# Three of twelve modulation blocks issued later, behind an output projection

## The chip, the cores and the metric

The kernel runs on one core of a Trainium2 chip. The metric is device time in microseconds (us) from launch to end; lower is better. A core has a matrix engine (TensorE, PE in the profile, with PEld for its weight loads), a vector engine (VectorE, DVE), a scalar engine (ScalarE, ACT), GpSimd (POOL) and SyncE (SP), which here issues nearly all DMAs. Each engine takes its instructions in the order in which the program lists them.

## What is computed

Two networks of two layers each on 256 rows of 1024 features. The first is causal attention and a gated convolutional MLP. The second takes the first one's result as `x` and a second sequence, the context, and each of its layers is modulated by six vectors of 1024 numbers, for the latent sequence (`ml`) and for the context (`mc`):

```python
for i in range(DEPTH):
    ml = jnp.split(s_lat @ w_ada[i] + b_ada[i], 6, axis=-1)
    mc = jnp.split(s_ctx @ w_ada[i] + b_ada[i], 6, axis=-1)
    u_lat = modulate(h_lat, g_pre_mix[i], ml[0], ml[1])
    ...
    h_lat = h_lat + ml[2] * rms_norm_2(o_lat, g_post_mix[i])
    f_lat = sqrelu_mlp(modulate(h_lat, g_pre_ff[i], ml[3], ml[4]), w_ff1[i], w_ff2[i])
    h_lat = h_lat + ml[5] * rms_norm_2(f_lat, g_post_ff[i])
```

`w_ada[i]` is 1024 by 6144, in float32. The vectors depend on two small inputs alone, so they can be made at any time before they are used.

## The kernel before

All large products are made in three passes of float32r: a weight tile (`raw`, 512 KB) is loaded by SP, ScalarE makes its high part (`whi`, L265), DVE or POOL the low part (`wlo`, L269), and TensorE multiplies. Matmuls write PSUM banks, of which there are four groups: A, B, C and D. D is one bank.

The method `ada` (L751 on) makes the modulation in twelve blocks of 512 columns. A block is eight loads of 256 KB (tile `adaw`, L775, on SP), eight matmuls (L778) whose left side is 32 columns wide, so that four of them use different column strips of the array, a copy to SBUF on ScalarE (`asb`, L780), four transposes (`adaT`, L784), and a reduction and an addition on DVE (L786, L787). The trace has two records for each of these float32 matmuls, 16 for a block. In the lane `sd`, which the change touches, the eight loads share six buffers (tag `mid`), and both PSUM tiles of a block use bank D, so blocks run one after another. The last of the three blocks (index 9) has two more small DVE instructions, which fold the norm's gain into its result.

Blocks 0 to 3 of the second layer serve its first norm, 4 and 5 its first gate, 6 to 9 the norm ahead of its MLP (shift and scale), 10 and 11 its last gate. `side` traces blocks 0 to 9 and then `setup_odd`, a table of biases made in eight steps (`chk` loads on POOL, transposing matmuls `cb`, L1097), in the lane `sd` too.

The program text is a priority list, not the order of issue. A planner fixes each engine's order ahead of the run, with a model of how long everything takes: of what is ready on an engine it takes what was traced first. Thus blocks traced ahead of the first network's second MLP (`conv_ffn(1)`) mix with it and with the steps around it. `behind(steps)` traces steps so that their TensorE instructions come after the last projection matmul traced so far (`self.last`) in TensorE's order. Nothing else of the steps is held by it; their DMAs start when a buffer is free.

In `run`, the order of tracing is: the first network's layer 0, the context's first mixer, blocks of layer 0's modulation, the first network's layer 1 attention, `side`, `conv_ffn(1)`, then `second_block`. In that, `lat_out` is an output projection followed by `post` (a scaled residual), `lat_mlp` a norm (`nT` transposes, L370) followed by an MLP of 16 steps (`f`, L308 to L310, and `acc`, L746 to L748). `context2` makes the context's projection and MLP beside the latent mixer and then its next norm, and blocks 10 and 11 already stand behind the second `lat_out`, in the lane `cx`.

```python
    def behind(self, steps):
        with self.tc.issue_after(self.last.ins):
            for _ in steps:
                pass
```

Of the kernel before, what the change touches and what calls it, by code (L numbers as in the profile page):

```python
# [188 lines left out]
class Net:  # L189
# [865 lines left out]
            pass  # L1055

    def side(self):
        for _ in itertools.chain(self.ada(self.sd, 1, 1, range(10)), self.setup_odd(self.sd)):
            pass

    def behind(self, steps):
# [85 lines left out]
    def rwkv_group(self, L, s, feat, put, ve, p0, n, tz, sg, vd, fill):  # L1147
# [86 lines left out]
        for pi in range(n):  # L1234
# [64 lines left out]
            for c in range(8):  # L1299
                for d in range(2):  # L1300
                    for h, hr in enumerate(hs):
                        nc.tensor.matmul(sc[h][hs[side(h, d)], c], BK[hr, d, c], AR[hr, d, c], start=True, stop=True)
# [5 lines left out]
            for h in range(2):  # L1308
                q0 = (pi * 2 * 2 + h) * 8
                nc.sync.dma_start(nm[q0:q0 + 8].rearrange("c s t -> s c t"), G[lows[h], h, :, 0:32])  # L1310
                o = lows[side(h, 1)]
                nc.vector.transpose(nt[o], G[o, h, :, 0:32])
                nc.sync.dma_start(nm[q0 + 16:q0 + 24].rearrange("c s t -> s c t"), nt[o])

            BG = L.mid([128, 2, 256], name="ic"), L.mid([128, 2, 256], name="kd")
            for d in range(2):
                step()
                bg = BG[d].rearrange("p a (c t) -> p (a c) t", t=64)
                nc.vector.tensor_tensor(bg, BK[:, d], gC[:, d, pi].unsqueeze(2).to_broadcast([128, 8, 64]), op=OP.mult)
                ps = L.pB("bkt")  # L1320
                pv = ps.rearrange("p (c f) -> p c f", c=4)
                for c in range(4):
                    nc.tensor.transpose(pv[:, c], bg[:, 2 * c:2 * c + 2].rearrange("p c t -> p (c t)"), self.ident)
                for e in range(2):
                    for h in range(2):
                        eng = nc.scalar.copy if e == 0 else nc.vector.tensor_copy
                        eng(BKt[hs[side(h, d)], d, e::2], pv[hs[e], :, hs[h]])
# [437 lines left out]
    def second_block(self, x):  # L1765
        L = self.lat
        end = self.last
        act = self.even_mix(L, 0, x)
        self.lat_out(0, act, x)
        odd = self.context2(end)  # L1770
        self.lat_mlp(0, x)
        self.behind(odd)
        act = self.odd_mix(x)
        self.lat_out(1, act, x)
        self.behind(self.ada(self.cx, 1, 2, range(10, 12)))
        self.lat_mlp(1, x)
# [62 lines left out]
```

## Time and profile before

| | us |
|---|---|
| Median of 3 runs (2070.97 to 2075.08) | 2072.32 |
| The profiled execution | 2065.47 |
| Its span, first to last instruction | 2063.3 |
| TensorE busy | 1898.4 (92%) |
| DVE busy | 1378.0 (67%) |
| ACT busy | 1026.3 (50%) |
| POOL busy | 852.4 (41%) |

The stages that matter, from the trace: the first network's last output projection ends at 741 us; the norm ahead of `conv_ffn(1)` lasts to 758.7; `conv_ffn(1)` runs to 996, with the context's recurrent scan beside it; the second block's mixer runs to 1435; its first `lat_out` ends at 1462.6; the norm of `lat_mlp(0)` lasts to 1485.8 and its matmuls to 1666. Blocks 7, 8 and 9 of the second layer's modulation run from 743.6 to 792. In the views, PEclk is the granted clock of TensorE as a share of its full 2.4 GHz, so 0.5 is 1.2 GHz; "x" is a count of records, and what stands in brackets behind "<-" ended an idle time.

### The profile page before, as it was taken

The page shows a single profiled execution, that of the slowest core. Times are in us where ns is not written, and L with a number is a line of the kernel's source. Part 1 is how long each engine was busy: PE and PEld are TensorE (multiplying, and loading weights), DVE is VectorE, ACT ScalarE, POOL GpSimd, SP SyncE. Part 2 cuts the span into 40 slices and gives each one's busy share as a digit, 9 for nine tenths or more (in the row PEclk, how much of TensorE's full clock was granted, in tenths as well). Part 3 has the DMA queues.
Part 4 walks back from the last instruction along what each step waited for, and adds up shares of the span by engine and source line. Part 5 has one row for each costly group of instructions (what it writes and reads, how often), then busy time and mean ns, then how long its engine had stood idle before and what let it go on. Part 6 is the DMA issues. An engine that isn't in the chain of part 4 may idle for free. (4 is left out here: it accounts for less than half of the span.)

```text
span 2063.3 us, 37705 instructions
## 1 busy us (share of the span) xinstructions
PE 1898.4 (92%) x14178; PEld 1580.8 (77%) x14178; DVE 1378.0 (67%) x2919; ACT 1026.3 (50%) x1990; POOL 852.4 (41%) x557
## 2 busy tenths in 40 slices
PE   6989999989999889999898888998699999998998
PEld 4567868888666458899797878887699977777997
DVE  5475378876788646786778888678744468645444
ACT  4455455545454335465555544554544444654443
POOL 3235544593332444454544433113255554013453
PEclk9999999999999999999999999999799999999999
DMA  9857555445454665575472653327555436225562
GB/s 344 311 176 229 159 171 168 146 153 178 127 191 160 199 196 171 183 232 170 133 255 95 184 152 117 91 61 215 183 174 195 164 100 232 82 93 164 180 198 72
DMA packets 270815, 351.08 MB, mean 170 GB/s; under 512 B 43150, under 2 KB 195469, under 8 KB 270632
## 3 DMA queue, kind: packets, MB, share of 16 engines
q1 hardware_dynamic: 267992, 343.32, 51.8%
q0 software_dynamic: 1968, 4.33, 0.7%
q8 instruction: 112, 1.84, 0.4%
q10 hardware_dynamic: 672, 1.02, 0.1%
q14 instruction: 71, 0.58, 0.1%
HBM read 334.04 MB, written 14.55 MB: 169 GB/s over the span
## 5 line engine op out<-in xcount | busy, mean ns | idle before, releaser
L269 POOL TENSOR_TENSOR wlo<-raw,whi 128x1024 fp32r<-128x1024 f32 (+2 forms) x344 | 705.3, 2061 | 1042.6 <-ACT whi L265 920.2
L265 ACT ACTIVATE whi<-raw 128x1024 fp32r<-128x1024 f32 (+2 forms) x600 | 508.2, 883 | 140.7 <-issue 34.0
L269 DVE TENSOR_TENSOR wlo<-raw,whi 128x1024 fp32r<-128x1024 f32 (+1 forms) x256 | 356.7, 1395 | 112.5 <-ACT whi L265 101.4
L310 PE MATMUL f<-ah,wlo 128*128 128x256 f32 x768 | 222.3, 290 | 13.5 <-DVE wlo L269 6.9
L308 PE MATMUL f<-ah,whi 128*128 128x256 f32 x768 | 220.6, 288 | 2.8 <-DVE T L1343 1.8
L309 PE MATMUL f<-al,whi 128*128 128x256 f32 x768 | 222.2, 290 | 0.0
L746 PE MATMUL acc<-whi,hh 128*128 128x512 f32 x432 | 168.8, 393 | 2.1 <-ACT hh L461 2.1
L747 PE MATMUL acc<-wlo,hh 128*128 128x512 f32 x432 | 169.3, 392 | 0.0
L748 PE MATMUL acc<-whi,hl 128*128 128x512 f32 x432 | 165.3, 390 | 0.4 <-DVE hl L462 0.4
L310 PEld LDWEIGHTS f<-ah,wlo 128*128 128x128 f32 x768 | 150.0, 195 | 17.2 <-DVE wlo L269 8.5
L308 PEld LDWEIGHTS f<-ah,whi 128*128 128x128 f32 x768 | 150.0, 196 | 5.7 <-ACT whi L265 2.5
L309 PEld LDWEIGHTS f<-al,whi 128*128 128x128 f32 x768 | 150.1, 196 | 2.9 <-issue 0.8
L1596 ACT ACTIVATE r<-f 128x512 f32<-128x512 f32 x48 | 28.6, 596 | 191.2 <-PE f L310 191.2
L1597 DVE TENSOR_TENSOR r<-r 128x512 f32<-128x512 f32 x48 | 34.6, 721 | 131.8 <-ACT r L1596 131.6
L293 PE MATMUL prj<-wlo,ah 128*128 128x512 f32 (+1 forms) x272 | 107.1, 395 | 2.7 <-DVE wlo L269 1.6
L292 PE MATMUL prj<-whi,ah 128*128 128x512 f32 (+1 forms) x272 | 107.4, 400 | 0.4 <-DVE bt L499 0.4
L310 PE MATMUL g<-ah,wlo 128*128 128x256 f32 x352 | 101.4, 288 | 5.8 <-POOL wlo L269 5.8
L294 PE MATMUL prj<-whi,al 128*128 128x512 f32 (+1 forms) x272 | 105.4, 396 | 1.2 <-DVE al L383 1.2
L778 PE MATMUL ada<-adaw,kept 128*32 128x512 f32 x384 | 98.8, 640 | 7.3 <-DMA adaw<-in_w_ada_dram 6.9
L308 PE MATMUL g<-ah,whi 128*128 128x256 f32 x352 | 101.9, 290 | 0.4 <-DVE kept L786 0.4
L308 PE MATMUL up<-ah,whi 128*128 128x256 f32 x352 | 102.2, 290 | 0.0
L310 PE MATMUL up<-ah,wlo 128*128 128x256 f32 x352 | 101.3, 288 | 0.9 <-POOL wlo L269 0.9
(473 smaller groups left out, 4825.8 us busy)
## 6 DMA issues: line engine op xcount, KB each, us to landing
raw<-in_w_ff_dram SPq DMA_DIRECT2D x128, 512.0 KB, 4.1
raw<-in_w_up_dram SPq DMA_DIRECT2D x88, 512.0 KB, 4.6
adaw<-in_w_ada_dram SPq DMA_DIRECT2D x144, 256.0 KB, 5.4
raw<-in_w_ff_dram SPq DMA_DIRECT2D x128, 256.0 KB, 4.6
raw<-in_w_in_dram SPq DMA_DIRECT2D x48, 512.0 KB, 4.7
raw<-in_w_down_dram SPq DMA_DIRECT2D x44, 512.0 KB, 4.5
adaw<-in_w_ada_dram SPq DMA_DIRECT2D x24, 512.0 KB, 7.6
raw<-in_w_out_dram SPq DMA_DIRECT2D x24, 512.0 KB, 5.1
```

Of the source, the lines that this page charges most:

```text
L265: nc.scalar.activation(hi, raw, AF.Copy)
L269: eng.tensor_tensor(lo, raw, hi.bitcast(F32), op=OP.subtract)
L292: nc.tensor.matmul(ps[t][:, :n], ah, wh[:, k], start=st, stop=False)
L293: nc.tensor.matmul(ps[t][:, :n], ah, wl[:, k], start=False, stop=False)
L294: self.last = nc.tensor.matmul(ps[t][:, :n], al, wh[:, k], start=False, stop=en)
L308: nc.tensor.matmul(pv[:, j], wh[:, k % a, c], ah, start=first, stop=False, skip_group_check=skip)
L309: nc.tensor.matmul(pv[:, j], wh[:, k % a, c], al, start=False, stop=False, skip_group_check=skip)
L310: nc.tensor.matmul(pv[:, j], wl[:, k % a, c], ah, start=False, stop=k == 7, skip_group_check=skip)
L746: nc.tensor.matmul(acc[t][n], hh[:, k, c], wh[:, n], start=st, stop=False)
L747: nc.tensor.matmul(acc[t][n], hh[:, k, c], wl[:, n], start=False, stop=False)
L748: self.last = nc.tensor.matmul(acc[t][n], hl[:, k, c], wh[:, n], start=False, stop=en)
L778: nc.tensor.matmul(ps[32 * j:32 * j + 32], self.sT[:, k], raw[:, k - kb], start=k < 4, stop=k >= 4)
```

## The change

`side` traces blocks 0 to 6 only, and blocks 7 to 9 are traced in `second_block` right after the first `lat_out`, through `behind`, in the same lane with the same buffers. No operation is added or removed.

```diff
     def side(self):
-        for _ in itertools.chain(self.ada(self.sd, 1, 1, range(10)), self.setup_odd(self.sd)):
+        for _ in itertools.chain(self.ada(self.sd, 1, 1, range(7)), self.setup_odd(self.sd)):
             pass
...
         act = self.even_mix(L, 0, x)
         self.lat_out(0, act, x)
+
+        self.behind(self.ada(self.sd, 1, 1, range(7, 10)))
         odd = self.context2(end)
         self.lat_mlp(0, x)
         self.behind(odd)
```

## Rows read from the trace of the kernel before

**Rows 1.** Stretch, length, busy time: PE, PEld, DVE, ACT, POOL; PEclk, DMA share, GB/s.
```profile
741.00:758.60 17.60, 11.13 (x52) 4.23 (x50) 11.14 (x30) 8.12 (x18) 7.18 (x12) 0.81 0.69 214
758.60:793.00 34.40, 34.40 (x311) 23.71 (x312) 15.77 (x40) 13.82 (x29) 6.60 (x6) 1.00 0.61 196
1462.00:1486.00 24.00, 7.88 (x36) 6.72 (x35) 20.36 (x73) 14.18 (x32) 4.00 (x2) 0.58 0.34 113
...
880.00:940.00 60.00, 58.29 (x405) 54.48 (x404) 50.69 (x68) 35.88 (x50) 29.72 (x14) 1.00 0.71 222
1486.00:1530.00 44.00, 44.00 (x301) 41.08 (x301) 23.42 (x27) 21.64 (x28) 22.48 (x8) 0.99 0.59 189
```

**Rows 2.** TensorE's waits from 758.7 to 996 us: total, times, longest.
```profile
PE acc L746 <- ACT hh L461: 1.7, 1, 1.7
PE yT L1465 <- DVE Y L1460: 1.7, 1, 1.7
...
```

**Rows 3.** Busy by stretch, `ada` alone: PE, PEld, ACT; clock, DMA share, GB/s.
```profile
758.60:793.00 34.40, 10.29 (x32) 1.50 (x32) 1.20 (x2) 1.00 0.61 196
```

**Rows 4.** The same, `adaT` alone (transposes, reductions): PE, PEld, DVE.
```profile
758.60:793.00 34.40, 1.20 (x8) 0.92 (x8) 0.56 (x3) 1.00 0.61 196
```

**Rows 5.** Timeline of TensorE around one matmul of block 8: start, length, what.
```profile
761.03 1.05 PE L778 MATMUL ada<-adaw,kept 128*32 128x512 f32 x2
762.01 0.38 PE L308 MATMUL g<-ah,whi 128*128 128x256 f32 x1
```

**Rows 6.** Timeline at the end of the norm at 741 to 758.7 us.
```profile
756.15 1.05 PE L778 MATMUL ada<-adaw,kept 128*32 128x512 f32 x2
757.13 0.66 PE L370 MATMUL nT<-kept,xn 128*128 128x128 f32 x4
757.88 0.66 PE L784 MATMUL adaT<-kept,asb 128*128 128x128 f32 x4
758.69 0.38 PE L308 MATMUL g<-ah,whi 128*128 128x256 f32 x1
```

**Rows 7.** Timeline of TensorE at the end of the later norm.
```profile
1479.02 0.69 PE L370 MATMUL nT<-kept,xn 128*128 128x128 f32 x2 [6.93 <-DVE xn L362]
1482.85 3.25 PE L370 MATMUL nT<-kept,xn 128*128 128x128 f32 x14 [3.15 <-DVE xn L362]
1485.75 0.56 PE L308 MATMUL f<-ah,whi 128*128 128x256 f32 x1
```

**Rows 8.** TensorE's waits from 1462.5 to 1486 us: total, times, longest.
```profile
PE nT L370 <- DVE xn L362: 16.1, 3, 6.9
```

**Rows 9.** DMAs that SP issued from 737 to 759 us (first and last).
```profile
737.25 9.21 SPq L263 DMA_DIRECT2D raw<-in_w_up_dram  x2
746.50 0.97 SPq L775 DMA_DIRECT2D adaw<-in_w_ada_dram  x2
...
758.17 0.45 SPq L775 DMA_DIRECT2D adaw<-in_w_ada_dram  x1
```

**Rows 10.** DMAs that SP issued in the later norm.
```profile
1468.81 0.50 SPq L818 DMA_DIRECT2D gate<-arow  x1
1477.20 15.64 SPq L263 DMA_DIRECT2D raw<-in_w_ff_dram  x6
...
1484.21 15.71 SPq L263 DMA_DIRECT2D raw<-in_w_ff_dram  x6
```

**Rows 11.** All 168 loads of the modulation's weights: time to landing.
```profile
DMA to landing us min/median/max: 2.7/5.6/10.8
```

**Rows 12.** A block's copy on ScalarE, then its DVE work at 1854 us.
```profile
L780 ACT ACTIVATE asb<-ada x4: 597/597/598, 742.4 to 788.6; 128x512 f32<-128x512 f32 x4
...
L786 DVE TENSOR_REDUCE kept<-adaT 128x8 f32<-128x32 f32 x2 | 0.4, 183 | 0.0
L787 DVE TENSOR_TENSOR kept<-kept 128x8 f32<-128x8 f32 x2 | 0.3, 160 | 0.0
```

**Rows 13.** Busy by stretch, the bias table's `cb` alone: PE, PEld, DVE.
```profile
800.00:880.00 80.00, 7.45 (x96) 5.04 (x96) 4.42 (x8) 1.00 0.61 181
```

## The prediction

> **What bounds the kernel now.** I read the busy time by stretch first, for the two places that the change touches. In the stretch that opens the first network's second MLP TensorE is busy for all of 34.4 us, while DVE has 15.8, ACT 13.8 and POOL 6.6 [rows 1]. The list of waits says the same for the whole MLP: from 758.7 to 996 us TensorE waited three times, 1.7 us each for the two longest, 3.8 us in all [rows 2]. So this stage ends when TensorE has done its work, and a microsecond of TensorE taken out of it is worth about a microsecond. The norm at 741 to 758.6 and the later one at 1462 to 1486 are the opposite. In the later one TensorE has 7.9 of 24 us to do, and DVE 20.4 [rows 1]; TensorE's waits there are 16.1 us, all for the DVE instruction that ends a scaling [rows 8]. Behind it comes `lat_mlp(0)`, where TensorE is again busy for all of 44 us [rows 1]. Hence the question: how much of the three blocks runs in the later norm, where TensorE is free, and how much falls into the MLP behind it, where it costs what it cost before.
>
> **What is removed, in the MLP at 758.7.** Blocks 8 and 9 lie in it, with 32 matmul records that are busy for 10.29 us [rows 3] and eight transposes with 1.20 us [rows 4]. They come in pieces, as their loads land: the timeline of the stretch has nine groups of these matmuls and two of transposes, of which [rows 5] show one. There the next matmul starts 0.98 us behind the block's own, whose record is 1.05 long, so 0.07 of each piece is shared. 10.29 + 1.20 less 11 times 0.07 gives 10.7 us of TensorE. Ends: 11.5, if nothing is shared, and 6.9, if TensorE's present 3.8 us of waits in this stage [rows 2] were to double, because weights then come too late. I take 10.7: in the stage's densest stretch DVE, which makes half of the low parts, is busy for 50.7 of 60 us [rows 1], so the supply has room.
>
> **What is removed, in the norm at 741.** Block 7 is there. Most of its matmuls run while TensorE has nothing to do. Two pieces stand in front of others: one matmul at 756.15, behind which the last four transposes start at 757.13, 0.98 later, and the block's own transposes at 757.88, which end as the MLP's first matmul starts at 758.69 [rows 6]. That is 0.98 + 0.7 = 1.7 us. Against it stands the clock. With the blocks in it this norm has a granted clock of 0.81, the later one without them 0.58 [rows 1], and there 14 transposes take 3.25 us and the first matmul `f` 0.56 [rows 7]. If the norm at 741 cools likewise, up to half of that 3.25, 1.6 us, is lost. I take 0.7, which leaves 1.0, with ends of 0.1 and 1.7.
>
> The Trainium skill (TensorE: Matmul & The Clock Gate, What's actually happening) has the half rate as the default, which activity lifts. By that rule the three blocks would also hold the clock up in the later norm, and with up to 1.6 us won there the sum below would be -6.6 instead of -5.0. No row shows that norm with work in it, so the sum leaves this out.
>
> **What moves with it.** `setup_odd` follows block 6 instead of block 9, some 45 us earlier. Its 96 matmul records, 7.45 us [rows 13], stay in the same TensorE-bound stage, and POOL, which issues its loads, is busy for 6.6 of 34.4 us there [rows 1]. I take nothing; one of its eight steps more or less in the norm is 0.9 us either way. On SP, 24 loads of 256 KB leave the stretch up to 778. Behind them stand weights and the small loads of the context's scan, which come earlier. The scan is hardly on the path: TensorE's one wait for it in this stage, ahead of its last transposes, is 1.7 us [rows 2]. The first six of the 24 find free buffers as soon as `setup_odd` is done near 880, long ahead of use.
>
> So the first place gives 10.7 + 1.0 = **11.7 us**.
>
> **What is added, behind the first `lat_out`.** TensorE's part may not start before 1462.6, and the next MLP starts at 1485.75 [rows 7]: 23.2 us. Six loads are there. The other 18 need a buffer that a matmul has released, then an issue on SP, then 5.6 us to land in the median, 10.8 at most [rows 11]. How many pass can be read from the norm at 741, which has the same lane, six buffers and an SP that also issues weights: between 741 and 758.7 SP issued eight of these loads, the first pair at 746.50, the last at 758.17 [rows 9]. In 23.2 us that rate gives 10.5. 6 + 10.5 is some 16 to 17 of 24 in the norm, and seven or eight, one block, in the MLP, in pieces as before: half of 10.7, or 5.4 us. On DVE the blocks add 3 times 0.18 and 0.16 [rows 12], and 0.3 for the last one's two small ones, 1.3 us on the engine that the norm waits for; all of it counts. The three copies on ACT are 0.6 us each [rows 12]; ACT has 14.2 of 24 us to do [rows 1], so I count none, 1.8 at the other end. Together **6.7 us**. Ends: a gain of 1.6, if all is done in the norm and the clock is held up for its 14 transposes, and a cost of 10.7 + 1.3 + 1.8 = 13.8.
>
> The sum is 6.7 - 11.7 = -5.0 us. The profiled execution took 2065.5, so a like one would take 2060.5; the median of the runs lies 6.9 above it, and on that I forecast 2072.3 - 5.0 = **2067.3 us**. The part between the two places is taken as shifted only. The planner arranges it anew, which I can't cost; I allow 2 us either way.
>
> **The rivals.** (B) All three blocks fit into the norm. For it: the room, 16.1 us of waits, against 10.7 us of pieces for two blocks. Against it: the rate of loads. Then only the 1.3 is left of the cost: -10.4, 2061.9 us.
>
> (C) The work is moved, not hidden: blocks 8 and 9 both fall into `lat_mlp(0)`, as they fell into the MLP before. For it: SP issues nothing for some 8 us in this norm, from 1468.8 to 1477.2 [rows 10], and a load listed behind such a wait is late whatever its own buffer does. 10.7 + 1.3 - 11.7 is +0.3, 2072.6 us: no change.
>
> (D) Slower: the blocks' matmuls hold the norm up. The planner's order puts them ahead of the norm's transposes, and SP's order puts their loads behind weights that wait for buffers. In this norm SP issues nothing between the gate's load at 1468.81 and 1477.20, and then waits again until 1484.21 [rows 10]. In the norm at 741 the like is seen: two weights take SP from 737.25 to 746.46, and the blocks' loads come behind them [rows 9]. A load issued behind the first lands at 1477.2 + 5.6 = 1482.8, and transposes that stand at 1479.02 [rows 7] would start 3.8 later; one behind the second lands at 1489.8, 7.0 later than the transposes at 1482.85. Both on top of the forecast are -5.0 + 10.8 = +5.8, 2078.1 us; the first alone gives 2071.1, so it takes both to end on the slower side. Against it: the block's matmuls at 756.15 stood ahead of transposes too, and their load was there.
>
> The Trainium skill (DMA: Bandwidth & Descriptors, Anatomy of one DMA) has a DMA's semaphore wait on the issuing sequencer, ahead of dispatch. That is what lets one waiting load hold up all that SP lists behind it; the trace agrees, as no load is issued inside those waits.
>
> (E) The change doesn't do what it is meant to: the MLP at 758.7 isn't shorter, because its pace is set by the supply of weights. -1.0 + 6.7 gives +5.7, 2078.0. Against it: 3.8 us of waits in 237 [rows 2].
>
> **How the numbers follow.** About 0.2%, 4.1 us, can be told from no change. The forecast has a chance of 0.48; with the clock, ACT's copies and the planner's 2 us it ends between -9 and 0, two thirds of it beyond -4.1: 0.32 faster, 0.16 same. B has 0.17, all faster. C has 0.18: 0.01 faster, 0.14 same, 0.03 slower. D has 0.13, 0.10 of it slower and 0.03 same. E has 0.04, slower. Sums: faster 0.50, same 0.33, slower 0.17. The range of 2060 to 2077 takes in B's time and C's, and leaves out most of D and E and the edge of B.
>
> **What would show it.** Right: the MLP from the norm's end to its last matmul is 10 to 11 us shorter; blocks 7 and 8 have their matmuls between the last of `lat_out` and the first `f`, block 9 among the `f`, in pieces of about 1 us; that norm is 1 to 2 us longer. Wrong towards B: no `adaw` matmul among the `f`. Towards C: two blocks among them. Towards D: TensorE waits for a load of `adaw` with transposes behind it, and the norm is over 27 us. Towards E: TensorE's waits in the first MLP grow by as much as was taken away. What would upset the whole sum is a change between 1000 and 1435 us, where the planner mixes two streams.

## The result: 28 us slower

The changed kernel took 2099.23 us in the median (2095.30 to 2102.86, 4 runs), the one before 2071.64 beside it (2060.84 to 2075.08, 4 runs): a ratio of 1.0142, 95% interval 1.0119 to 1.0165. The forecast was 2067.3, the range 2060 to 2077. The profiled execution of after took 2102.86, its span 2101.1; that of before 2065.47 and 2063.3.

The first table cuts both spans at TensorE's own marks: the last `wo` of the second layer, the first `g`, the last `acc` of the first network, the last `lo` of the first `lat_out`, the first `f` behind it. The two profiled executions are 37.8 us apart, 10 more than the medians, so a line of the table can be off by a few us. Of the 37.8, 18.7 lie ahead of everything that the edit touches. By TensorE's account 20.5 of them are more busy time for the same 14,178 matmul records (1918.9 us against 1898.4), and 17.3 are more standing.

| stretch | before | after | difference | forecast |
|---|---|---|---|---|
| start to last `wo` | 741.3 | 760.0 | +18.7 | 0 |
| norm, to first `g` | 17.4 | 19.4 | +2.0 | -1.0 |
| first network's MLP | 238.0 | 235.3 | -2.7 | -10.7 |
| to the last `lo` | 465.8 | 469.0 | +3.2 | 0 |
| later norm, to first `f` | 23.2 | 30.8 | +7.6 | +6.7, some of it behind the norm |
| the rest | 577.6 | 586.6 | +9.0 | 0 |

Busy time by stretch in the kernel after; the columns are those of [rows 1], and the stretches answer to the norm, the MLP's start, its middle, the later norm and the start of `lat_mlp(0)` there.

```profile
760.00:779.40 19.40, 7.04 (x41) 4.79 (x39) 13.72 (x32) 7.84 (x18) 13.46 (x23) 0.63 0.46 123
779.40:814.00 34.60, 34.60 (x385) 30.95 (x385) 22.15 (x44) 14.55 (x30) 14.32 (x15) 0.96 0.51 139
901.00:961.00 60.00, 56.76 (x395) 53.22 (x394) 48.63 (x61) 33.61 (x45) 26.66 (x12) 0.97 0.66 206
1483.70:1514.50 30.80, 24.33 (x92) 7.87 (x93) 23.38 (x78) 16.38 (x38) 5.54 (x2) 0.89 0.74 239
1514.50:1558.50 44.00, 43.17 (x296) 40.05 (x295) 23.88 (x27) 20.18 (x26) 16.36 (x7) 1.00 0.45 134
```

Of the kernel after, the same view for `ada` alone in the later norm (PE, PEld, ACT), for [rows 3], and for `adaT` alone (PE, PEld, DVE), for [rows 4].

```profile
1483.70:1514.50 30.80, 17.64 (x48) 2.59 (x48) 1.80 (x3) 0.89 0.74 239
...
1483.70:1516.00 32.30, 1.89 (x12) 1.31 (x12) 0.56 (x3) 0.89 0.70 228
```

All 48 matmul records of the three blocks stand in the later norm; the forecast had a third of them among the `f`. The norm at 760 has lost block 7 and is still 2.0 us longer, at a granted clock of 0.63 instead of 0.81.

TensorE's waits in the kernel after (total, times, longest): in its MLP from 779.4 to 1014.6 us, for [rows 2], and below the dots in its later norm, for [rows 8].

```profile
PE yT L1465 <- DVE Y L1460: 3.2, 1, 3.2
PE acc L746 <- ACT hh L461: 2.1, 1, 2.1
...
PE ada L778 <- DMA adaw<-in_w_ada_dram: 2.4, 3, 0.9
PE nT L370 <- DVE xn L362: 2.4, 1, 2.4
PE ada L778 <- ACT mod L381: 1.3, 1, 1.3
```

The timeline of TensorE in the kernel after: the end of the norm at 760 us, for [rows 6], and below the dots the end of the later norm, for [rows 7] (start, length, what, and in brackets the idle time ahead).

```profile
773.59 0.42 PE L370 MATMUL nT<-kept,xn 128*128 128x128 f32 x1
777.91 1.55 PE L1097 MATMUL cb<-fl,chk 128*64 128x128 f32 x12 [3.90 <-DMA chk<-rpb_line]
779.39 0.58 PE L308 MATMUL g<-ah,whi 128*128 128x256 f32 x1
...
1508.74 1.73 PE L778 MATMUL ada<-adaw,kept 128*32 128x512 f32 x4 [0.89 <-DMA adaw<-in_w_ada_dram]
1510.40 0.87 PE L370 MATMUL nT<-kept,xn 128*128 128x128 f32 x6
1511.20 2.09 PE L778 MATMUL ada<-adaw,kept 128*32 128x512 f32 x6
1513.22 1.09 PE L370 MATMUL nT<-kept,xn 128*128 128x128 f32 x8
```

SP's DMAs in the kernel after around the later norm, for [rows 10].

```profile
1473.75 12.45 SPq L263 DMA_DIRECT2D raw<-in_w_ff_dram  x4
1486.25 0.91 SPq L775 DMA_DIRECT2D adaw<-in_w_ada_dram  x2
1489.40 2.61 SPq L263 DMA_DIRECT2D raw<-in_w_ff_dram  x2
1492.06 15.55 SPq L775 DMA_DIRECT2D adaw<-in_w_ada_dram  x16
```

Two local readings. Ahead of the MLP's first `g` stand 12 matmul records of `setup_odd`, which wait 3.90 us for a load. In the later norm the order puts the blocks' matmuls between the transposes, and their loads behind four weights that take SP 12.45 us, its waits included.

The rest isn't local. The section on the kernel before says that the planner takes of what is ready what was traced first; that is too simple. Compared engine by engine, without the three blocks' own 71 instructions, the two programs differ from the 27th TensorE instruction on, although the edit is traced long behind it: of the 11,884 pairs of neighbours on TensorE 707 are others, on DVE 446 of 2814, on ACT 226 of 1763, on SP 135 of 1069, on POOL 68 of 552. What comes later in the program weighs in what is put first. So one edit made two changes: three blocks in another place, and another order of all the rest. The layout of tiles in SBUF, which is found anew for each program, turned out to be a third.

### The profile page after: what moved, and what is told of

Same layout as the page of the kernel before. It is cut to its first block, busy times and chain, and to the rows that moved or that the text cites. A ratio compares the mean times of both kernels' runs of the same rounds, so it can differ in the third digit from the quotient of the medians.

```text
span 2101.1 us, 37688 instructions
## 1 busy us (share of the span) xinstructions
PE 1918.9 (91%) x14178; PEld 1590.7 (76%) x14178; DVE 1398.8 (67%) x2919; ACT 1034.4 (49%) x1990; POOL 823.6 (39%) x557
## 5 line engine op out<-in xcount | busy, mean ns | idle before, releaser
L269 POOL TENSOR_TENSOR wlo<-raw,whi 128x1024 fp32r<-128x1024 f32 (+2 forms) x344 | 678.3, 1978 | 1124.6 <-ACT whi L265 915.1
L265 ACT ACTIVATE whi<-raw 128x1024 fp32r<-128x1024 f32 (+2 forms) x600 | 519.4, 886 | 394.7 <-PE f L309 91.6
L269 DVE TENSOR_TENSOR wlo<-raw,whi 128x1024 fp32r<-128x1024 f32 (+1 forms) x256 | 311.1, 1216 | 264.2 <-ACT whi L265 248.4
L1597 DVE TENSOR_TENSOR r<-r 128x512 f32<-128x512 f32 x48 | 92.7, 1930 | 29.0 <-ACT r L1596 28.8
L309 PE MATMUL g<-al,whi 128*128 128x256 f32 x352 | 103.0, 293 | 0.0
L309 PE MATMUL up<-al,whi 128*128 128x256 f32 x352 | 101.6, 289 | 0.0
```

The costliest lines, as they stand in the source:

```text
L265: nc.scalar.activation(hi, raw, AF.Copy)
L269: eng.tensor_tensor(lo, raw, hi.bitcast(F32), op=OP.subtract)
L309: nc.tensor.matmul(pv[:, j], wh[:, k % a, c], al, start=False, stop=False, skip_group_check=skip)
```

## The experiments

Place and order can be separated. The order of every instruction but those 71 was read off a built program and tied up in the kernel: each instruction is to be issued behind its neighbour on its engine. The tie is one of order alone (`NoSync`) and asks for no semaphore. Whichever way the blocks are then traced, all else keeps its order; the blocks themselves are free.

```diff
+    how = mybir.DependencyInfo(mybir.DependencyClass.NoSync, mybir.DependencyReason.DATA)
...
+        for a, b in zip(line, line[1:]):
...
+            tc.add_manual_dep(own[b], own[a].name, how, reason="hold_order")
```

All ratios below are to the kernel before, run beside them, with 95% intervals of 0.0014 to 0.0036 either way; 0.001 is 2.1 us, and a difference of two ratios is good to 0.003, to 0.005 where both kernels have four runs. The stretches come from one profiled execution each, in us. The last three kernels are planned freely. In behind_mlp_free and late_loads_free `f` matmuls stand inside the later norm; there it is counted to the `f` that follow it, and the last two columns are to be read as a sum.

| run | ratio | start to `wo` | norm | MLP | to `lo` | later norm | rest |
|---|---|---|---|---|---|---|---|
| hold_before | 1.0033 | 742.0 | 17.1 | 243.5 | 467.4 | 25.7 | 580.8 |
| moved_order_before | 1.0029 | 751.0 | 15.0 | 227.9 | 463.9 | 32.1 | 584.4 |
| old_place_order_after | 1.0143 | 754.9 | 29.2 | 234.1 | 468.4 | 28.3 | 582.1 |
| hold_after | 1.0142 | 758.6 | 19.2 | 234.5 | 468.8 | 30.7 | 585.8 |
| left_out | 0.9947 | 741.6 | 14.1 | 227.1 | 461.7 | 27.3 | 577.5 |
| behind_mlp | 0.9980 | 742.2 | 14.1 | 226.3 | 480.0 | 23.4 | 577.5 |
| moved_more_room | 0.9977 | 746.1 | 14.1 | 226.2 | 463.4 | 31.8 | 577.4 |
| moved_late_loads | 0.9932 | 738.1 | 14.0 | 226.9 | 468.6 | 24.7 | 576.8 |
| after_late_loads | 1.0090 | 755.0 | 17.1 | 234.1 | 471.6 | 28.5 | 577.9 |
| sp_order_after | 1.0051 | 760.9 | 14.2 | 226.2 | 472.9 | 27.9 | 580.4 |
| te_order_before | 1.0128 | 765.7 | 15.4 | 234.0 | 471.6 | 31.4 | 582.5 |
| late_sp_order_after | 1.0048 | 753.5 | 14.1 | 227.3 | 470.2 | 30.3 | 580.3 |
| late_te_order_before | 0.9976 | 749.3 | 14.5 | 229.2 | 464.2 | 23.6 | 580.3 |
| behind_mlp_free | 1.0100 | 742.4 | 19.4 | 229.5 | 477.0 | 49.3 | 569.0 |
| late_loads_free | 1.0092 | 748.1 | 20.2 | 236.2 | 467.9 | 55.3 | 565.4 |
| spare_1024 | 1.0053 | 749.1 | 17.1 | 238.2 | 470.5 | 27.2 | 579.6 |

**The place and the order, each alone.** Two kernels hold the order of before, two that of after; in each pair one has the blocks in the old place and one in the new.

> Control: the kernel before, with the order of all instructions but those of blocks 7, 8 and 9 written down and held on every engine as the kernel before has it; the three blocks stand where they stood and are free. Every theory expects the time of before, 2072 us within 4 us. If it is off by more, holding an order itself costs something (or where tiles lie in SBUF does), and the next three are compared with this one.

> The change alone: blocks 7 to 9 queued behind the first output projection, while all other instructions keep on every engine the order of the kernel before. Theory O (the 30 us outside the norm and the two MLPs come from the planner's other order of the whole program, the blocks' own move costs the 7 us seen in its three stages): 2065 to 2081 us, the first 740 us as in before within 2 us, the later norm 28 to 32 us. Theory L (the move itself does it, through what the blocks hold or wait for in the stages between): 2095 to 2103. Theory S (tiles lie closer in SBUF, since six weight buffers are held from 850 to 1480 us, and writers wait for the last readers of their bytes): also about 2095 to 2103, with the loss spread over the stages ahead of 740 us too.

> The converse: blocks 7 to 9 in their old place in the source, while all other instructions keep on every engine the order that the changed kernel has. Theory O: 2088 to 2100 us, with the first 740 us 13 to 19 us longer than in before. Theory L and theory S: 2068 to 2076, as before.

> Control: the changed kernel with its own order on every engine held, all instructions in the same order; only the places of tiles in SBUF are found anew. Theories O and L: 2099 us within 4 us. Theory S expects that another placement can move it by more than 5 us.

Measured: 2077.13, 2075.79, 2099.43 and 2096.91 us. With the layout that each kernel gets, moving the blocks does nothing that can be told, in either order (-0.0004 and -0.0001). The other order costs 0.0110 with the blocks in the old place and 0.0113 in the new, 23 us. That is theory O: most of after's loss is the order's. Two things are off. The held kernel before is itself 7 us slower than the free one. All else has its order, but the blocks, being free, stand elsewhere in the queues; the largest piece is in the MLP, 243.5 us instead of 238.0, where TensorE stands for 6.2 instead of 3.8 and is busy 3.0 longer. Why was not tried. And moved_order_before reaches the last `wo` 9 us late, though all that stands ahead of it keeps its order. The busy time by stretch up to there, of hold_before and then of moved_order_before:

```profile
0.00:742.00 742.00, 673.44 (x4518) 516.28 (x4522) 485.06 (x1173) 369.62 (x760) 331.91 (x274) 0.97 0.59 193
```

```profile
0.00:751.00 751.00, 681.73 (x4518) 519.08 (x4522) 493.28 (x1173) 373.30 (x759) 328.21 (x274) 0.96 0.59 188
```

The same 4518 matmul records are busy for 8.3 us more, at a granted clock of 0.96 instead of 0.97: by the traces' clock records TensorE is at 1.2 GHz for 58 us of this stretch instead of 41. No single wait accounts for that.

**What the blocks cost.**

```diff
-        self.behind(self.ada(self.sd, 1, 1, range(7, 10)))
+        self.moved.add(self.nc.vector.memset(self.adac[1][:, :, 28:40], 1.0).ins.name)
```

> Blocks 7 to 9 of the second layer's modulation are left out (their 12 columns are filled with ones by one write), all other instructions keep the order of the kernel before: what the three blocks cost at all. If the old place costs what the prediction said (11.7 us), and the new place 6.7: 2065 us against 2077 of the held kernel before, and 7 under the kernel with the move alone (2076 would have been 2072). If the move alone gained nothing because the blocks were nearly free in the old place: 2074 or more. If old and new place cost the same, the gap to both is one number, 8 to 14 us.

```diff
-        act = self.even_mix(L, 0, x)
+        self.behind(self.ada(self.sd, 1, 1, range(7, 10))); act = self.even_mix(L, 0, x)
         self.lat_out(0, act, x)
...
-        self.behind(self.ada(self.sd, 1, 1, range(7, 10)))
```

> Blocks 7 to 9 queued behind the first MLP instead of behind the first output projection; all other instructions keep the order of the kernel before. They then run among the matmuls from 1000 to 1090 us, where TensorE is busy for 21 to 25 of every 25 us. If a block costs its matmuls wherever TensorE is the bound: as the held kernel before, 2074 to 2079. If the waits of that stretch hide them: 2064 to 2070.

Measured: 2057.52 and 2065.81 us. left_out has ones in place of what the blocks make. It is 0.0086 faster than the held kernel before, 18 us, more than was expected; 16.4 of it is in the MLP (243.5 to 227.1) and 3.0 in the norm. Against the free kernel before it is 0.0053, 11 us, near the 11.7 of the forecast: the other 7 come with the places that the blocks have in the held control. Behind the MLP the blocks cost 0.0033, 7 us; the stretch to `lo` grows by 12.6 against the held kernel and the MLP falls by 17.2. That fits the expectation that the waits there hide part of the work.

**Layout and loads.** Six loads of the moved blocks go out early, in after between 849 and 858 us and in moved_order_before between 874 and 885, while their matmuls come past 1457 in both. Their buffers, 2 KB of each partition apiece, are held all that time, and tiles that had these bytes must lie elsewhere.

```diff
-            nc.sync.dma_start(raw[p], ap)
+            self.load = nc.sync.dma_start(raw[p], ap)
...
-        self.behind(self.ada(self.sd, 1, 1, range(7, 10)))
+        with self.tc.issue_after(self.load.ins):
+            self.behind(self.ada(self.sd, 1, 1, range(7, 10)))
```

> The move with the order of the kernel before held on every engine, as in the second run, but SP issues all 24 weight loads of blocks 7 to 9 behind the last weight load of the first output projection (in the second run six of them went out near 850 us and held their buffers to 1480). Theory S (those six buffers crowd SBUF, tiles lie so that writers wait for readers of the same bytes all over the program): TensorE reaches the end of the second wo at 742 us as in the held kernel before, not at 751, and the median falls from 2076 to 2063 to 2070, with the later norm 0 to 3 us longer, since no load is there ahead. Without theory S (the 9 us were chance or come from the blocks themselves): 2073 to 2080, 749 to 753.

```diff
-KEPT = 7168
+KEPT = 7040
```

> The second run again, the same instructions in the same order on every engine and the six early loads as well, but the kept lane is 7040 instead of 7168 numbers wide, which gives the tiles' layout 512 bytes more per partition and another result. Theory S: 2063 to 2070, end of the second wo at 742. Theory H (it is the six loads themselves, early in SP's queue, that cost): 2073 to 2080.

> The changed kernel in its own order on every engine, with the 24 loads behind the last weight load of the first output projection. Theory S with theory O: 9 us less than the held changed kernel, 2084 to 2092, since the other order still costs its share. Theory O alone: 2094 to 2100. If the early loads were the whole cause: 2063 to 2072.

Measured: 2052.76, 2062.22 and 2086.89 us. With the same instructions in the same order on every engine, 512 bytes more for the layout are worth 0.0052, 11 us, so the layout is a cost of its own (theory S). The last `wo` came at 746.1, though, not at 742. The traces tell two kinds of layout apart, best by the 48 squarings `r<-r` on DVE. Here they are in moved_order_before and in moved_more_room: busy time, mean ns, idle time ahead.

```profile
L1597 DVE TENSOR_TENSOR r<-r 128x512 f32<-128x512 f32 x48 | 92.9, 1934 | 24.0 <-ACT r L1596 23.9
```

```profile
L1597 DVE TENSOR_TENSOR r<-r 128x512 f32<-128x512 f32 x48 | 34.6, 722 | 129.4 <-ACT r L1596 129.3
```

In the first trace 39 of the 48 run beside an instruction of GpSimd, in the second 7; those that run alone take 0.68 to 0.69 us in both. With no order changed, ScalarE's records name 2586 semaphore waits in the first and 2249 in the second: who waits for whom depends on the layout, and with it what runs beside what. How much of the 11 us goes which way stays open. after, hold_after and te_order_before have the first kind of layout, all the other kernels the second.

So the two pairs above compare like with like for the order (hold_before and old_place_order_after have the second kind, moved_order_before and hold_after the first), but not for the place. From hold_before to moved_more_room, both of the second kind, the move gains 0.0056, 12 us; the layout that comes with it in moved_order_before takes 0.0052 back.

Holding the loads back gives 0.0045 more than moved_more_room, 9 us; whether by the loads or by smaller differences of layout stays open. In after's order late loads and the second kind of layout together give 0.0052. moved_late_loads, at 0.9932 (0.9904 to 0.9959), lies below all that was expected, beats both kernels, and equals the kernel without the blocks (0.9947): in the later norm they cost nothing that can be told, to some 6 us.

The later norm in moved_late_loads: busy time by stretch, TensorE's waits, and SP's DMAs for the blocks.

```profile
1447.60:1472.30 24.70, 18.59 (x89) 6.59 (x88) 20.27 (x79) 14.71 (x33) 3.35 (x1) 0.93 0.65 225
```

```profile
PE nT L370 <- DVE xn L362: 3.3, 2, 2.4
PE adaT L784 <- ACT asb L780: 1.7, 2, 1.5
PE ada L778 <- DMA adaw<-in_w_ada_dram: 1.1, 1, 1.1
```

```profile
1401.04 6.53 SPq L775 DMA_DIRECT2D adaw<-in_w_ada_dram  x6
1438.53 1.54 SPq L775 DMA_DIRECT2D adaw<-in_w_ada_dram  x2
1450.39 2.87 SPq L775 DMA_DIRECT2D adaw<-in_w_ada_dram  x6
1453.83 7.93 SPq L775 DMA_DIRECT2D adaw<-in_w_ada_dram  x10
```

TensorE has 18.6 us of work in 24.7 where it had 7.9 in 24.0 [rows 1], and its waits for `xn` fell from 16.1 [rows 8] to 3.3. SP issued the 18 later loads from 1438.5 to 1461.8, 9 us ahead of the last `lo` to 14 behind it. In after it was 3 to 24 us behind it, since four weights had SP first.

**Which order.** In two kernels SP has the order of after and the other engines that of before; in two TensorE alone is held, in the order of before, and the rest is planned anew. TensorE's order of after under the other engines' of before, and the other engines' of after under SP's of before, were not run.

> The change, with SP's queue (the weight loads) held to the order of the changed kernel and the four engines to that of the kernel before. If the other order of the loads costs the 20 us: 2090 to 2100. If it is the engines' order: 2071 to 2079, as the move alone.

> The change, with TensorE alone held to the order of the kernel before; the planner arranges SP and the other engines anew around it (a third order of theirs, neither that of before nor of after). If TensorE's order costs the 20 us: 2071 to 2080. If it is the loads' or the other engines' order that costs whenever it is planned anew: 2088 to 2100.

> The move with its 24 loads late, the four engines in the order of the kernel before, SP's queue in the order of the changed kernel. Base is 2053 us with SP's order of before, 2087 with every order of the changed kernel. If SP's order is half of it, as the run with early loads suggested (2079 against 2062): 2064 to 2072. If nearly all: 2080 to 2088. If nothing: 2050 to 2056.

> The move with its 24 loads late and TensorE alone in the order of the kernel before; SP, VectorE, ScalarE and GpSimd are planned anew around it. Base 2053 us with all held, 2087 in the changed kernel's order. If TensorE's order carries the cost: 2050 to 2058. If the loads' and the other engines' order carries it: 2070 to 2085.

Measured: 2079.12, 2095.86, 2080.32 and 2067.59 us. On the base of moved_late_loads SP's order alone costs 0.0116, 24 us of the 33 that after's whole order costs there (0.0158). sp_order_after, with early loads, shows less: 0.0074 against moved_more_room, which has its kind of layout, and 0.0022 against moved_order_before, which has the other. Holding TensorE's order doesn't keep the cost away: with the rest planned anew it is still 0.0044 with late loads, where 47 of SP's pairs of neighbours are others, and 0.0099 over moved_order_before with early ones, where 92 are. So where layouts are of one kind the queue of loads carries half to three quarters of what the order costs; what is left to the engines on the base with late loads, 0.0042, can hardly be told from nothing. late_te_order_before fits neither of its two expectations.

One place where SP's order costs can be seen at 680 to 700 us, in the second layer's attention. First SP's DMAs in moved_late_loads, then in late_sp_order_after, then TensorE's timeline in the latter.

```profile
679.88 1.74 SPq L1371 DMA_DIRECT2D uv<-vd  x4
682.06 1.78 SPq L775 DMA_DIRECT2D adaw<-in_w_ada_dram  x4
683.93 0.38 SPq L1310 DMA_DIRECT2D nm<-G  x1
```

```profile
687.88 1.74 SPq L1371 DMA_DIRECT2D uv<-vd  x4
690.49 0.90 SPq L1310 DMA_DIRECT2D nm<-G  x2
691.63 0.30 SPq L1313 DMA_DIRECT2D nm<-nt  x1
692.05 0.86 SPq L775 DMA_DIRECT2D adaw<-in_w_ada_dram  x2
```

```profile
689.30 1.04 PE L778 MATMUL ada<-adaw,kept 128*32 128x512 f32 x2 [0.27 <-DMA adaw<-in_w_ada_dram]
695.30 2.53 PE L778 MATMUL ada<-adaw,kept 128*32 128x512 f32 x4 [4.96 <-DMA adaw<-in_w_ada_dram]
```

In the first order four loads of `adaw` follow the `uv` and then the small loads of the scan; in the second the scan's stand first and wait for their data, the `adaw` behind them is issued at 692.05, and TensorE, whose next instruction needs it, stands for 4.96 us. The stage from the last projection to the last `wo`, as busy time by stretch: moved_late_loads, late_sp_order_after, and of the latter the part behind the wait, with PE's busy time alone ahead of clock, DMA share and GB/s.

```profile
663.20:738.10 74.90, 66.15 (x398) 41.98 (x400) 43.92 (x129) 32.15 (x82) 41.98 (x59) 0.98 0.58 189
```

```profile
671.60:753.50 81.90, 70.12 (x398) 43.39 (x397) 43.08 (x128) 32.44 (x82) 42.45 (x59) 0.92 0.55 173
```

```profile
695.30:715.00 19.70, 16.75 (x89) 0.70 0.77 230
```

The same 398 matmul records are busy for 70.1 us instead of 66.2, and behind the wait the granted clock is 0.70 over 20 us, some 12 of them at 1.2 GHz: the stretch is 7.0 longer, 4.0 of it by slower matmuls and 3.0 by standing. These are 7.0 of the 26.6 us between the two traces; 8.4 more lie ahead of this stretch and 5.6 in the later norm, which were not followed. The Trainium skill (DMA: Bandwidth & Descriptors, Anatomy of one DMA) has the wait of a DMA on its issuing sequencer; the trace agrees, nothing passes SP from 689.6 to 690.49.

**Any other plan.**

> Blocks 7 to 9 queued behind the first MLP, and no order held: the planner arranges the whole program anew, a third order. If every new order costs some 20 us against the one of the kernel before, which would then be an unusually good one: 2085 to 2095. If the changed kernel's order is an unlucky one: 2062 to 2072, as with the order held (2066).

> The move with its 24 loads late and nothing else held: what one would get by writing it so. If the cost of a new plan is common (three of three so far were 20 to 30 us over the held order): 2070 to 2090. If it was bad luck: 2053 to 2062.

> The kernel before with its kept lane 8192 instead of 7168 numbers wide; nothing reads or writes the 1024 more. No work is moved; the planner's order changes in some places all the same (210 of TensorE's 11884 neighbour pairs; the changed kernel has 707 others). If any other plan costs: 2078 to 2095. If the size of the change in order counts: 2070 to 2080. If only the edit's own plan is bad: 2067 to 2071.

Measured: 2087.93, 2092.91 and 2080.83 us, ratios 1.0100, 1.0092 and 1.0053. The same edits with before's order held took 0.9980 and 0.9932, so the plans that these edits get cost 25 and 33 us, some 17 and 19 of it from the later norm on: 618 and 621 us there against 601 in behind_mlp and 601.5 in moved_late_loads. late_loads_free is slower than either of its expectations. Even 1024 numbers that nothing uses cost 11, by order or layout, which were not told apart; 210 of TensorE's pairs of neighbours are others there. Together with after's, each of the four plans of a whole kernel is worse than before's. Why they all are isn't settled: a model that ranks them otherwise than the chip, or a plan of before that happens to be good, would look alike here.

## Why the prediction was wrong, point by point

**The step that failed** is "The part between the two places is taken as shifted only", with its 2 us either way. Outside the stages that I costed the sum had no other term, and none at all for what stands ahead of 741 us. The new order measured 23 us with the blocks in either place, and 33 with the loads late; the layout that came with the early loads measured 11. An account on the kernel before, from the ratios: other places of the blocks in the held control +6.8, the move in the second kind of layout -11.6, the first kind of layout +10.8, the order +23.4: +29.4, which is 1.0142. The last sentence of the prediction named a change between 1000 and 1435 us as what would upset the sum; by the traces it came everywhere, half of it ahead of 741.

**The move itself** was forecast well. With before's order and its kind of layout it came out at 0.9977, -4.8 us against the kernel before, where -5.0 was forecast: MLP -11.8, norm -3.3, later norm +8.6 (moved_more_room). That the sum fits so closely is in part luck: with late loads the same move gave -14.

**The MLP, -10.7.** The mechanism was right. Against the trace of before it measured -10.1 (238.0 to 227.9) with the order held, against the held kernel -15.6. In after it came to -2.7. Every kernel with the whole of after's order takes 234 to 235 us there, with the blocks moved or not (old_place_order_after 234.1, with the blocks in the norm). The stage as busy time by stretch, in moved_order_before and in after:

```profile
766.00:993.90 227.90, 224.21 (x2032) 202.28 (x2032) 160.44 (x286) 121.52 (x195) 99.03 (x64) 1.00 0.61 187
```

```profile
779.40:1014.60 235.20, 228.88 (x2023) 205.70 (x2022) 169.37 (x280) 119.65 (x191) 96.97 (x57) 0.98 0.60 183
```

Of the 7.3 us between them 4.7 are busy time, at a granted clock of 0.98 instead of 1.00, and 2.6 are standing.

**The norm at 741, -1.0.** With the order held -2.1 to -3.1 against the held kernel, and in after +2.0.

**`setup_odd`, 0.** Not its place among the steps but its load cost: 3.90 us of waiting ahead of the first `g`, in the norm of after. It comes with after's order: with the order of before no kernel waits there. I had looked at how busy POOL was, not at what TensorE would find first in its queue.

**The later norm, 6.7.** The size was near, +7.6, by luck, since it came another way. I had one block in the MLP behind it, from the rate of loads in another norm; in fact all three are in the norm, as in rival B, and hold it up, as in rival D: 30.8 us, over D's mark of 27, with TensorE waiting three times for `adaw`. What I read as the lane's rate was SP's order: with the same buffers and the 18 loads some 11 us earlier against the last `lo` the norm is 24.7, and with SP's order of after and all else as there 30.3 (late_sp_order_after).

**The clock.** The first place of the Trainium skill in the prediction (TensorE: Matmul & The Clock Gate, What's actually happening) has activity lift the half rate, by which the blocks would hold the clock up in the later norm. The trace agrees: 0.89 in after and 0.93 with late loads, against 0.58 without them [rows 1]. What that gave back was not measured by itself.

**The rivals.** C and E had no part in it: in after no block's matmuls stand among the `f`, and with the order of before held the MLP was shorter by what was taken out. In after TensorE's waits in the MLP grew from 3.8 to 6.3 us, E's sign in part, but none of them was for weights. None of the rivals was a new order of the whole program, to which I gave no chance; the 0.17 for slower was made of D, E and an edge of C.

## What to carry to other kernels

Where a planner fixes the order, compare the two programs' orders first: if they differ ahead of the edit, the edit's own cost is not what will be measured. Hold the order of the kernel before, see that the layout of tiles stays of one kind, and move only the work: with late loads that gave -14 us on the kernel before, where the same edit planned freely gave +19. Of a step that is moved, look where its loads stand in the issuing queue and how long their buffers are held.

## What the hardware showed that was not expected

With all instructions in the same order, another layout of tiles moved the time by 11 us (1.0029 to 0.9977). A squaring on DVE took 0.68 us alone and 2.22 on the mean beside GpSimd (moved_order_before). The stretch with TensorE's wait of 5 us was 7.0 us longer, 4.0 of it by slower matmuls, with a granted clock of 0.70 over the 20 us behind the wait. And the later norm took in three blocks, 18.6 us of busy TensorE instead of 7.9, with no cost that could be told, once their loads were there.
